# A hybrid attention block with fewer, wider transfers, eight places for the raw differential values, and broadcasts finished later

## The chip, the cores and the metric

The kernel runs on one core of a Trainium2 chip. TensorE (PE) multiplies; VectorE (DVE), ScalarE (ACT) and GpSimd (POOL) do the element-wise work; SyncE (SP) only issues DMAs, and ACT issues some too. Each engine works through its own list of instructions in order and waits on semaphores. The metric is the device time of one execution in microseconds (us), the median of three runs. Times inside an execution are microseconds from the start of the profiled span.

## The reference

The block works on one sequence of 1024 rows and 1024 channels, all float32. One input norm and one wide projection feed two attention branches, which gates merge:

```python
h = rms_norm(x, norm_in); proj = h @ w_in
(dq, dk, dv, dgate, cq, ckv, kr, mgate, g_diff, g_mla) = jnp.split(proj, split_idx, axis=-1)
# differential branch: 4 heads, two maps of 64 each, values 128 wide
dq, dk = apply_rope(dq), apply_rope(dk)
o_diff = causal_multimap_attention(dq, dk, dv, [1, -lam], 64 ** -0.5)
o_diff = rms_norm(o_diff, diff_subln) * (1 - lambda_init) * silu(dgate)
# latent branch: 4 heads, 128 + 64 rope; cq is 384 wide, ckv 256
q = rms_norm(cq, mla_q_norm) @ w_uq;  kv = rms_norm(ckv, mla_kv_norm) @ w_ukv
o_mla = causal_multimap_attention(concat(q_nope, rope(q_rope)), concat(k_nope, rope(kr)), mv) * silu(mgate)
merged = sigmoid(g_diff) * (o_diff @ w_proj_diff) + sigmoid(g_mla) * (o_mla @ w_proj_mla)
return rms_norm(x + merged @ w_out, norm_final)
```

## The kernel before, in words

Every product of two float32 matrices is made of three matmuls (`mm3`, L158 to L161): each operand is split into a rounded high part and the remainder as a low part (`split`, L150: ACT casts, then DVE or POOL subtracts), and high×high, high×low and low×high are summed in PSUM.

**Start, 0 to 67 us.** The raw differential values are made first: eight steps over blocks of 128 channels (order `KORD`), each with 24 matmuls into eight PSUM banks (`psd`, L216). After the last step each bank is copied by ACT into a tile of the tag `t`, which has four places (L391, L392), and stored by a DMA that ACT issues too (`d_dr`, L393). The rows of x are loaded meanwhile (`load_row`, L302) and squared on ACT for the input norm.

**Units, 67 to 486 us.** The rest of the wide projection is 19 units (`unit`, L470), each of which makes two column blocks of 128 for all 1024 rows by Strassen's seven products of 12 matmuls. `weights` (L342) builds the seven combinations of a unit's weights from four raw tiles (`wr`, loaded at L339; six places). The results go through sinks: rotation and split and store (`sink_rope`), gates (`sink_gate`, `sink_silu`), raw latent columns (`sink_c`). `store_split` (L562) writes the high part into a tile `uh` and the low part into `ul`, with two places each, and stores each by a DMA of its own. Between the products *chores* are called from a list: rope tables of one half (`rope_half`, L678), blocks of the differential values (`dv_block`, L724), and the latent norm's scaling (`latent_norm`, L632). A row of scale factors is broadcast over the partitions by `spread` (L613): POOL writes a diagonal into a `uh`, `ul` pair, and 9000 ns of the program's own count later (`defer`, L630) PE multiplies it by ones into the bank `tp`. That happens for the input norm's two halves (`rbc`) and for four latent jobs.

**Heads, 486 us to the end.** `load_stacks` (L879) loads a differential head's queries and keys as six tiles of 128 partitions, by twelve DMAs of 64 partitions each; `load_dv` (L891) loads its values and gate. Then come scores, softmax and the product with the values; the latent branch's tiles (`ch`, `cl`, `cosm`, `sinm`, `krh`, `krl`, L1001 on) are loaded after the first head's. The merge, the output projection and the last norm end the kernel.

A scheduler lays out the instructions of each engine from this program before it runs; the order in a queue is therefore not the order of the lines. The DMAs of SP and ACT share eight completion semaphores (`DMAHW0` to `DMAHW7`) in turn. A DMA whose semaphore still belongs to an earlier DMA is issued only after that one has landed, and the issuing engine's later instructions stand behind it.

## Time and profile before

| | us |
|---|---|
| median of 3 runs (955.65 to 956.18) | 955.98 |
| the profiled execution | 959.97 |
| its span | 958.2 |
| PE busy in it | 870.7 |
| DVE busy | 658.1 |
| POOL busy | 431.3 |
| ACT busy | 391.6 |

The profiled execution is 1.77 us longer than its span. PE is busy in 91% of the span, at a mean granted clock of 0.954 of full speed; a busy PE is not always a PE at full clock, so a stretch is read by its busy time and its granted clock together. In a row of waits, "A <- B" reads: A stood idle until B was done. In the timeline an idle time ahead of an instruction and what ended it stand in brackets.

### The profile page before, as it was taken

Reading aid. Unit: us, or ns where it says so; the run is one execution under the profiler, and the core shown is the slowest. Engines: PE = TensorE matmul, PEld = TensorE weight load, DVE = VectorE, ACT = ScalarE, POOL = GpSimd, SP = SyncE. Lnnn points to the kernel's source line nnn. Section 1 sums busy time; section 2 is a strip of 40 time slices with the busy share of each in tenths; the row PEclk is TensorE's granted clock in tenths of the full one; section 3 lists DMA queues with packets and bytes.
Section 4 is the critical chain, followed back from the end, with each engine's and each line's share of the span. In section 5 each row is a group of like instructions: output and inputs, shape, how many; then the busy total and the mean of one; then the engine's idle time right before and its main releaser. Section 6 shows DMA issues by size and latency. Waiting matters only on the chain.

```text
span 958.2 us, 12234 instructions
## 1 busy us (share of the span) xinstructions
PE 870.7 (91%) x4100; PEld 713.1 (74%) x4100; DVE 658.1 (69%) x1080; ACT 391.6 (41%) x768; POOL 431.3 (45%) x345
## 2 busy tenths in 40 slices
PE   8939899978798999999948899997999889999997
PEld 6727688756576878888835688886889658888886
DVE  7928666899989798866527568688587557554242
ACT  7563443233242333344315356565465443222211
POOL 6755345866756665545406533436243722220001
PEclk9969999979988999999978799999999999999999
DMA  7362332479583333332379621634131357444051
GB/s 275 115 242 77 110 113 96 133 230 283 200 270 136 108 134 119 123 111 99 95 205 383 151 72 63 148 104 123 49 122 55 109 175 232 134 132 165 19 182 64
DMA packets 71967, 137.92 MB, mean 144 GB/s; under 512 B 7904, under 2 KB 18912, under 8 KB 71904
## 3 DMA queue, kind: packets, MB, share of 16 engines
q1 hardware_dynamic: 64704, 124.16, 41.0%
q10 hardware_dynamic: 7200, 12.98, 3.7%
q8 instruction: 32, 0.52, 0.2%
q14 instruction: 31, 0.25, 0.1%
HBM read 91.76 MB, written 45.35 MB: 143 GB/s over the span
## 4 chain that ended last, share of the span: by engine, by line
PE 50%; DVE 5%; DMA 4%; ACT 3%; POOL 1%; issue 1%; SPq 0%; POOLq 0%; DVEq 0%; ACTq 0%
PE mm L159 9%; PE mm L161 9%; PE mm L160 9%; PE acc L161 3%; PE acc L159 3%; PE acc L160 3%; PE pv L160 2%; DVE sc L815 2%; PE mm L833 2%; PE sc L919 1%; PE pv L161 1%; PE pv L159 1%; PE sc L920 1%; DMA or<-d_od 1%; PE sc L1115 1%
## 5 line engine op out<-in xcount | busy, mean ns | idle before, releaser
L152 POOL TENSOR_TENSOR wl<-ws,wh 128x512 fp32r<-128x512 f32 x57 | 83.6, 1476 | 80.3 <-ACT wh L151 50.0
L815 DVE CUSTOM_DVE_ANT_0 sc<-sc,mask 128x128 f32<-128x128 f32 (+7 forms) x96 | 72.7, 763 | 30.6 <-PE sc L920 16.8
L152 POOL TENSOR_TENSOR wl<-wr,wh 128x512 fp32r<-128x512 f32 x45 | 64.0, 1421 | 36.9 <-ACT wh L151 32.0
L352 POOL TENSOR_TENSOR ws<-wr,wr 128x512 f32<-128x512 f32 x38 | 56.8, 1495 | 43.4 <-issue 22.2
L151 ACT CAST wh<-ws 128x512 fp32r<-128x512 f32 x76 | 46.8, 618 | 66.8 <-PE mm L160 61.6
L817 ACT ACTIVATE e<-sc,mn 128x128 f32<-128x128 f32 (+3 forms) x64 | 47.6, 745 | 34.2 <-DVE mn L815 22.5
L151 ACT CAST uh<-c 128x512 fp32r<-128x512 f32 x35 | 21.6, 619 | 88.0 <-DVE c L559 44.6
L159 PE MATMUL acc<-woh,mh 128*128 128x512 f32 (+1 forms) x136 | 51.3, 377 | 0.0
L161 PE MATMUL acc<-woh,ml 128*128 128x512 f32 (+1 forms) x136 | 51.3, 377 | 0.0
L160 PE MATMUL acc<-wol,mh 128*128 128x512 f32 (+1 forms) x136 | 51.3, 377 | 0.0
L152 POOL TENSOR_TENSOR wpl<-wpr,wph 128x512 fp32r<-128x512 f32 x16 | 21.8, 1365 | 62.2 <-ACT wph L151 62.2
L151 ACT CAST wh<-wr 128x512 fp32r<-128x512 f32 x64 | 39.5, 617 | 23.8 <-PE mm L160 11.5
L919 PE MATMUL sc<-kh,qs 128*128 128x512 f32 (+2 forms) x96 | 39.0, 410 | 11.1 <-DMA kh<-d_qk 8.2
L931 POOL TENSOR_SCALAR eb<-eb,rs 128x128 f32<-128x128 f32 (+5 forms) x24 | 17.1, 711 | 67.7 <-DVE rs L927 53.7
L159 PE MATMUL mm<-b11h,wh 128*128 128x512 f32 x76 | 33.1, 436 | 14.8 <-ACT t L392 14.8
L1129 POOL TENSOR_SCALAR e<-e,rs 128x128 f32<-128x128 f32 (+5 forms) x24 | 16.6, 696 | 56.4 <-DVE rs L1125 52.8
L1319 POOL TENSOR_TENSOR r<-s,nhalf 128x1 f32<-128x1 f32 x7 | 3.8, 544 | 83.9 <-DVE s L1317 81.7
L833 PE MATMUL mm<-ident,e 128*128 128x128 f32 x200 | 37.0, 281 | 2.7 <-DVE part L1210 1.2
L152 DVE TENSOR_TENSOR ul<-c,uh 128x512 fp32r<-128x512 f32 x35 | 36.5, 1045 | 3.7 <-DMA d_qk<-ul 1.8
L352 DVE TENSOR_TENSOR ws<-wr,ws 128x512 f32<-128x512 f32 x19 | 25.6, 1346 | 18.5 <-POOL wl L152 18.5
L920 PE MATMUL sc<-kl,qs 128*128 128x512 f32 (+2 forms) x96 | 34.3, 364 | 4.3 <-DMA kl<-d_qk 4.3
L152 DVE TENSOR_TENSOR pl<-mm,ph 128x512 fp32r<-128x512 f32 (+2 forms) x56 | 34.0, 610 | 5.7 <-ACT ph L151 5.3
(337 smaller groups left out, 2937.6 us busy)
## 6 DMA issues: line engine op xcount, KB each, us to landing
wr<-in_w_t SPq DMA_DIRECT2D x76, 256.0 KB, 3.0
d_t<-c ACTq DMA_DIRECT2D x32, 256.0 KB, 2.1
tg<-d_t SPq DMA_DIRECT2D x32, 256.0 KB, 3.0
big<-in_x SPq DMA_DIRECT2D x8, 512.0 KB, 5.6
d_qk<-uh SPq DMA_DIRECT2D x16, 256.0 KB, 2.3
d_qk<-ul SPq DMA_DIRECT2D x16, 256.0 KB, 2.6
qs<-d_qk SPq DMA_DIRECT2D x16, 256.0 KB, 6.1
kh<-d_qk SPq DMA_DIRECT2D x16, 256.0 KB, 6.9
```

Of the source, the lines that this page charges most:

```text
L151: A.copy(hi, src)
L152: (eng or V).tensor_tensor(lo, src, f32(hi), op=ALU.subtract)
L159: T.matmul(ps, lhsT=lh, rhs=rh, start=first, stop=False, skip_group_check=skip)
L160: T.matmul(ps, lhsT=lh, rhs=rl, start=False, stop=False, skip_group_check=skip)
L161: T.matmul(ps, lhsT=ll, rhs=rh, start=False, stop=last, skip_group_check=skip)
L352: eng.tensor_tensor(t, p_, q, op=op)
L815: V.tensor_tensor_reduce(sc[:, 0:W], sc[:, 0:W], mask[:, S - W:S], scale=-scale, scalar=BIG, op0=ALU.add, op1=ALU.min, accum_out=mn)
L817: A.activation(dst, sc[:, 0:W], AF.Exp, scale=-1.0, bias=mn, accum_out=sm)
L833: T.transpose(tp[:, blk(j)], pr[j][:, blk(kb)], ident)
L919: T.matmul(sc[:, c0:c0 + n], lhsT=q, rhs=kh[m][:, c0:c0 + n], start=True, stop=False)
L920: T.matmul(sc[:, c0:c0 + n], lhsT=q, rhs=kl[m][:, c0:c0 + n], start=False, stop=True)
L931: G.tensor_scalar(eb[:, 0:W], eb[:, 0:W], r, 0.0, op0=ALU.mult, op1=ALU.add)
```

## The change

Transfers are merged. Two blocks of `w_dv` and both halves of a `w_t` weight come by one DMA each into `wr` tiles of twice the width, three places in the place of six. The high and the low part of a result lie side by side in one tile `uhl` (two places), and one DMA stores both, in DRAM layouts that keep them together (`d_c`, `d_q`, `d_k`, `d_dv`, `d_rope`). A head's queries and keys come by six DMAs of 512 KB, its values by one, its gate by one; the latent tiles by one each for high and low. SP's list goes from 430 to 318 rows.

The list of PSUM banks of the first stage is reversed. Copies 4 to 7 of the raw values go into tiles of the tag `c` (six places), so that the eight copies have eight places. The subtraction for `s4` stands two steps earlier in `weights`. The second half of a broadcast is deferred by 13000 in the place of 9000. The count of instructions on PE, DVE, ACT's arithmetic and POOL stays the same but for the order.

```diff
-    d_dv = [one(dram, [4, P, NB - 1, P], F32, f"d_dv{i}") for i in range(2)]
-    d_df = one(dram, [4, P, 2, P], F32, "d_df")
+    d_dv = one(dram, [4, P, 16, P], F32, "d_dv")
     d_dr = one(dram, [NB, P, 512], F32, "d_dr")
-    d_c = [one(dram, [6, P, S], F32, f"d_c{i}") for i in range(2)]
+    d_c = [one(dram, [P, 2, S], F32, f"d_c{i}") for i in range(6)]
     d_cr = one(dram, [5, P, S], F32, "d_cr")
-    d_qk = [one(dram, [4, P, S], F32, f"d_qk{h}") for h in range(4)]
+    d_qk = [[one(dram, [P, 2, S], F32, f"d_{x}{h}") for x in "qk"] for h in range(4)]
     d_dg = one(dram, [4, P, S], F32, "d_dg")
-    d_rope = one(dram, [2, P, S], F32, "d_rope")
+    d_rope = one(dram, [P, 2, S], F32, "d_rope")
     d_od = one(dram, [4, P, S], F32, "d_od")
...
-    psd = [mk(ps0, [P, 512], F32, "bank", 8) for _ in range(NB)]
+    psd = [mk(ps0, [P, 512], F32, "bank", 8) for _ in range(NB)][::-1]
...
-    def load_x(k):
-        wr = mk(pw, [P, 512], F32, "wr", 6)
+    wrs = {}
+
+    def load_wd(i):
+        wrs[i] = mk(pw, [P, 2, 512], F32, "wr", 3)
+        return wrs[i]
+
+    def load_x(s):
+        k = KORD[s]
         xt = mk(p0, [P, S], F32, "big", 6)
...
+            if s % 2 == 0:
+                nc.sync.dma_start(load_wd(s // 2), a["w_dv"][s // 2::4].rearrange("k p c -> p k c"))
...
+        return wrs[s // 2][:, s % 2], xt
+
+    loaded = [load_x(s) for s in range(5)]
     V.memset(ones, 1.0)
...
-    def load_w_raw(u, which):
+    def load_w_raw(u, i):
         if u < len(plan):
-            for i, hf in which:
-                t = mk(pw, [P, 512], F32, "wr", 6)
-                nc.sync.dma_start(t.rearrange("p (k c) -> p k c", k=4), a["w_t"][plan[u][i]][:, 4 * hf:4 * hf + 4])
-                raw_w[u, i, hf] = t
+            t = raw_w[u, i] = mk(pw, [P, 2, 512], F32, "wr", 3)
+            nc.sync.dma_start(t.rearrange("p h (k c) -> p (h k) c", k=4), a["w_t"][plan[u][i]])
...
         for u in range(len(plan)):
-            a11, a21, a22, a12 = (raw_w.pop((u, *x)) for x in ((0, 0), (1, 0), (1, 1), (0, 1)))
-            load_w_raw(u + 1, ((0, 0), (1, 0)))
+            w1, w2 = (raw_w.pop((u, i)) for i in range(2))
+            a11, a12, a21, a22 = w1[:, 0], w1[:, 1], w2[:, 0], w2[:, 1]
+            load_w_raw(u + 1, 0)
             yield out("b11", a11, V)
...
             yield out("t2", s2, G)
+            s4 = new(a12, s2, ALU.subtract, V)
             yield out("b21", a12, G)
             s3 = new(a11, a21, ALU.subtract, G)
-            load_w_raw(u + 1, ((1, 1), (0, 1)))
+            load_w_raw(u + 1, 1)
             yield out("t3", s3, G)
...
             yield out("t4", a22, G)
-            s4 = new(a12, s2, ALU.subtract, V)
             yield out("b22", s4, V)
...
             if s == KD - 1:
-                raw = tmp()
+                raw = tmp() if b < 4 else mk(pst, [P, 512], F32, "c", CB)
                 last_copy[0] = A.copy(raw, psd[b]).ins
...
             all_chores()
-            load_w_raw(0, ((0, 0), (1, 0), (1, 1), (0, 1)))
+            load_w_raw(0, 0)
             for b in range(2):
...
             all_chores()
+            load_w_raw(0, 1)
             chores.extend([lambda b=b: square_row(b) for b in range(2)])
...
-    def store_split(src, hi_d, lo_d):
-        hi = mk(pst2, [P, 512], F32R, "uh", 2)
-        lo = mk(pst2, [P, 512], F32R, "ul", 2)
-        split(hi, lo, src)
-        nc.sync.dma_start(hi_d, f32(hi))
-        nc.sync.dma_start(lo_d, f32(lo))
-
-    def sink_rope(hi_d, lo_d):
+    def pair_tile():
+        return mk(pst2, [P, 2, 512], F32R, "uhl", 2)
+
+    def store_split(src, dst, eng=None):
+        hl = pair_tile()
+        split(hl[:, 0], hl[:, 1], src, eng)
+        nc.sync.dma_start(dst, f32(hl))
+
+    def sink_rope(dst):
         def sink(n, src, owned):
...
             def last():
-                store_split(box["g"], hi_d[:, half(n)], lo_d[:, half(n)])
+                store_split(box["g"], dst[:, :, half(n)])
                 drop()
...
         fl = mk(pst2, [P, 4], F32R, "fl", 2)
-        dg = [mk(pst2, [P, 512], F32R, x, 2) for x in ("uh", "ul")]
+        hl = pair_tile()
+        dg = [hl[:, i] for i in range(2)]
         fn = f[:, 4 * n:4 * n + 4]
...
             use(b)
-        defer(9000, finish)
+        defer(13000, finish)
...
             V.tensor_scalar(r, r, rstd[:, b:b + 1], None, op0=ALU.mult)
+            rv = r.rearrange("p (h c) -> p h c", h=4)
             if b % 4 == 3:
-                nc.sync.dma_start(d_df[:, :, b // 4, :].rearrange("h p c -> p h c"), r.rearrange("p (h c) -> p h c", h=4))
+                nc.sync.dma_start(d_dv[:, :, 14 + b // 4, :].rearrange("h p c -> p h c"), rv)
             if b < NB - 1:
-                hi = mk(pst2, [P, 512], F32R, "uh", 2)
-                lo = mk(pst2, [P, 512], F32R, "ul", 2)
-                split(hi, lo, r)
-                for i, v in enumerate((hi, lo)):
-                    nc.sync.dma_start(d_dv[i][:, :, b, :].rearrange("h p c -> p h c"),
-                                      f32(v).rearrange("p (h c) -> p h c", h=4))
+                hl = pair_tile()
+                split(hl[:, 0], hl[:, 1], r)
+                for i in range(2):
+                    nc.sync.dma_start(d_dv[:, :, 7 * i + b, :].rearrange("h p c -> p h c"),
+                                      f32(hl[:, i]).rearrange("p (h c) -> p h c", h=4))
             drop()
...
     def load_stacks(h):
-        st, kh, kl = stacks[h] = [[mk(pD, [P, S], F32R, f"{x}{m}", 1) for m in range(2)] for x in ("qs", "kh", "kl")]
-        src = d_qk[h]
-        for m in range(2):
-            own, other = slice(64 * m, 64 * m + 64), slice(64 - 64 * m, 128 - 64 * m)
-            nc.sync.dma_start(f32(st[m][own]), src[0][own])
-            nc.sync.dma_start(f32(st[m][other]), src[1][own])
-            for t, s_ in ((kh, src[2]), (kl, src[3])):
-                nc.sync.dma_start(f32(t[m][own]), s_[own])
-                nc.sync.dma_start(f32(t[m][other]), s_[own])
+
+        q = mk(pD, [P, 2, S], F32R, "qs", 1)
+        k = mk(pD, [P, 2, 2, S], F32R, "ks", 1)
+        for x in range(2):
+            r = slice(64 * x, 64 * x + 64)
+            nc.sync.dma_start(f32(q[r]), d_qk[h][0].rearrange("(m r) i s -> i r m s", m=2)[x])
+            for i in range(2):
+                nc.sync.dma_start(f32(k[r, i]), d_qk[h][1].rearrange("(m r) i s -> i r m s", m=2)[i])
+        stacks[h] = [[t[:, m] for m in range(2)] for t in (q, k[:, 0], k[:, 1])]
 
     def load_dv(h):
-        vh = mk(pD, [P, NB - 1, P], F32R, "dvh", 1)
-        vl = mk(pD, [P, NB - 1, P], F32R, "dvl", 1)
-        vf = mk(pD, [P, 2, P], F32, "dvf", 1)
-        nc.sync.dma_start(f32(vh), d_dv[0][h])
-        nc.sync.dma_start(f32(vl), d_dv[1][h])
-        nc.sync.dma_start(vf, d_df[h])
-        dvs[h] = vh, vl, vf
+        v = mk(pD, [P, 16, P], F32R, "dv", 1)
+        nc.sync.dma_start(f32(v), d_dv[h])
+        dvs[h] = v[:, 0:7], v[:, 7:14], f32(v[:, 14:16])
+        u = mk(pD, [P, S], F32, "du", 1)
+        nc.sync.dma_start(u, d_dg[h])
         for g in range(2):
-            dgate[h, g] = mk(pD, [P, 512], F32, "du", 2)
-            nc.sync.dma_start(dgate[h, g], d_dg[h][:, half(g)])
+            dgate[h, g] = u[:, half(g)]
...
     pL = pool("pL", "left")
-    cos = one(pL, [P, S], F32, "cosm")
-    sin = one(pL, [P, S], F32, "sinm")
-    ch = [one(pL, [P, S], F32R, f"ch{c}") for c in range(5)]
-    cl = [one(pL, [P, S], F32R, f"cl{c}") for c in range(5)]
-    krh = one(pM, [P, S], F32R, "krh")
-    krl = one(pM, [P, S], F32R, "krl")
+    rope = one(pL, [P, 2, S], F32, "rope")
+    cos, sin = rope[:, 0], rope[:, 1]
+    chl = [one(pL, [P, 2, S], F32R, f"chl{c}") for c in range(5)]
+    ch, cl = ([t[:, i] for t in chl] for i in range(2))
+    krhl = one(pM, [P, 2, S], F32R, "krhl")
+    krh, krl = krhl[:, 0], krhl[:, 1]
...
-    def load_c(c):
-        for t, d in ((ch, d_c[0]), (cl, d_c[1])):
-            nc.sync.dma_start(f32(t[c]), d[c])
-
-    load_c(3)
-    load_c(4)
+    for c in (3, 4):
+        nc.sync.dma_start(f32(chl[c]), d_c[c])
     load_latent_w(0)
-    nc.sync.dma_start(f32(krh), d_c[0][5])
-    nc.sync.dma_start(f32(krl), d_c[1][5])
     for c in range(3):
-        load_c(c)
-    nc.sync.dma_start(cos, d_rope[0])
-    nc.sync.dma_start(sin, d_rope[1])
+        nc.sync.dma_start(f32(chl[c]), d_c[c])
+    nc.sync.dma_start(f32(krhl), d_c[5])
+    nc.sync.dma_start(rope, d_rope)
```

ACT's list at the end of the first stage, before, with what each instruction waits for (`bank` are the PSUM banks, `t` the four places, `big` the rows of x):

```order
62 L392 COPY t_573<-bank_170 128x512 [waits PE_49]
63 L392 COPY t_583<-bank_171 128x512 [waits PE_49]
64 L392 COPY t_589<-bank_172 128x512 [waits DMAHW3_49,PE_49]
65 L393 DMA d_dr<-t_573 128x512 [waits DMAHW6_49,Activation_49]
66 L393 DMA d_dr<-t_583 128x512 [waits DMAHW7_49,Activation_49]
67 L393 DMA d_dr<-t_589 128x512 [waits DMAHW0_49,Activation_49]
68 L151 CAST wh_648<-ws_642 128x512 [waits PE_49,Pool_49]
69 L392 COPY t_595<-bank_173 128x512 [waits DMAHW5_49]
70 L393 DMA d_dr<-t_595 128x512 [waits DMAHW1_49,Activation_49]
71 L392 COPY t_601<-bank_174 128x512 [waits DMAHW6_49]
72 L392 COPY t_607<-bank_175 128x512 [waits DMAHW7_49]
```

The copies in rows 64, 69, 71 and 72 wait for a DMA semaphore, that of the store that empties their place. After, where `bank_181` to `bank_174` are the same eight results in the same order, ACT's list reads:

```order
62 L403 COPY t_566<-bank_179 128x512 [waits PE_49]
63 L403 COPY t_576<-bank_178 128x512 [waits PE_49]
64 L404 DMA d_dr<-t_566 128x512 [waits DMAHW6_49,Activation_49]
65 L404 DMA d_dr<-t_576 128x512 [waits DMAHW7_49,Activation_49]
66 L403 COPY c_582<-bank_177 128x512 [waits PE_49]
67 L403 COPY c_588<-bank_176 128x512 [waits PE_49]
68 L403 COPY c_594<-bank_175 128x512 [waits PE_49]
69 L404 DMA d_dr<-c_582 128x512 [waits DMAHW1_49,Activation_49]
70 L404 DMA d_dr<-c_588 128x512 [waits DMAHW2_49,Activation_49]
71 L404 DMA d_dr<-c_594 128x512 [waits DMAHW3_49,Activation_49]
72 L403 COPY c_600<-bank_174 128x512 [waits PE_49]
```

The copies of the fifth to eighth bank no longer wait for a DMA semaphore; the stores of the third and the fourth stand ahead of them and wait for `DMAHW6` and `DMAHW7`.

DVE's list in the second unit, before (`r` are tiles of the rope table's second half, L484 and L488 two sums of the unit):

```order
83 L684 CAST r_250_1063<-r_252_1065 128x512
84 L152 TENSOR_TENSOR wl_932<-ws_929,wh_931 128x512
85 L685 TENSOR_SCALAR r_249_1062<-r_250_1063,ropec 128x512
86 L687 TENSOR_SCALAR r_251_1064<-r_249_1062 128x512
87 L688 TENSOR_SCALAR r_251_1064<-r_251_1064 128x512
88 L484 TENSOR_TENSOR u_945<-mm_900,u_882 128x512
89 L690 SCALAR_TENSOR_TENSOR r_249_1062<-r_251_1064,r_249_1062 128x512
90 L152 TENSOR_TENSOR wl_965<-wr_746,wh_964 128x512
91 L692 SCALAR_TENSOR_TENSOR r_250_1063<-r_251_1064,r_249_1062 128x512
92 L488 TENSOR_TENSOR c_977<-mm_947,u_945 128x512
```

The CAST stands nine rows ahead of the sum of L488. DVE's list there after (L495, L499 and L504 are L484, L488 and L493 of before):

```order
82 L495 TENSOR_TENSOR u_910<-mm_888,u_870 128x512
83 L362 TENSOR_TENSOR ws_991<-wr_737,ws_966 128x512
84 L152 TENSOR_TENSOR wl_926<-wr_737,wh_925 128x512
85 L499 TENSOR_TENSOR c_951<-mm_912,u_910 128x512
86 L725 TENSOR_TENSOR crs<-r_213_948,rbc 128x512
87 L727 TENSOR_TENSOR srs<-r_214_949,rbc 128x512
88 L504 TENSOR_TENSOR c_980<-mm_953,u_910 128x512
89 L697 CAST r_246_1093<-r_248_1095 128x512
90 L698 TENSOR_SCALAR r_245_1092<-r_246_1093,ropec 128x512
91 L700 TENSOR_SCALAR r_247_1094<-r_245_1092 128x512
```

The conversion of the positions (CAST) and what follows it stood ahead of the unit's sums and now stands behind them.

SP's list at the first head, before:

```order
226 L884 DMA qs_988_4165<-d_qk_82 64x1024 [waits DMAHW1_49]
227 L885 DMA qs_988_4165<-d_qk_82 64x1024 [waits DMAHW2_49]
228 L887 DMA kh_990_4167<-d_qk_82 64x1024 [waits DMAHW3_49,PE_49]
229 L888 DMA kh_990_4167<-d_qk_82 64x1024 [waits DMAHW4_49]
230 L887 DMA kl_992_4169<-d_qk_82 64x1024 [waits DMAHW6_49]
231 L888 DMA kl_992_4169<-d_qk_82 64x1024 [waits DMAHW7_49]
232 L884 DMA qs_989_4166<-d_qk_82 64x1024 [waits DMAHW0_49]
233 L885 DMA qs_989_4166<-d_qk_82 64x1024 [waits DMAHW1_49]
234 L887 DMA kh_991_4168<-d_qk_82 64x1024 [waits DMAHW2_49]
235 L888 DMA kh_991_4168<-d_qk_82 64x1024 [waits DMAHW3_49]
236 L887 DMA kl_993_4170<-d_qk_82 64x1024 [waits DMAHW4_49]
237 L888 DMA kl_993_4170<-d_qk_82 64x1024 [waits DMAHW5_49]
```

Every one of the twelve waits for the landing of the DMA that last had its semaphore. SP's list there after (`ks` holds what `kh` and `kl` held):

```order
157 L898 DMA qs_4019<-d_q_84 64x2x1024 [waits DMAHW4_49,PE_49]
158 L900 DMA ks_4020<-d_k_85 64x2x1024 [waits DMAHW5_49]
159 L900 DMA ks_4020<-d_k_85 64x2x1024 [waits DMAHW6_49]
160 L898 DMA qs_4019<-d_q_84 64x2x1024 [waits DMAHW7_49]
161 L900 DMA ks_4020<-d_k_85 64x2x1024 [waits DMAHW1_49]
162 L900 DMA ks_4020<-d_k_85 64x2x1024 [waits DMAHW2_49]
163 L905 DMA dv_4027<-d_dv 128x2048 [waits DMAHW3_49,PE_49]
```

Twelve loads have become six of twice the size, each with a wait for one semaphore of the eight.

## Rows read from the trace of the kernel before

**Rows 1.** The page, part 1: busy us, share of the span, instructions
```profile
PE 870.7 (91%) x4100; PEld 713.1 (74%) x4100; DVE 658.1 (69%) x1080; ACT 391.6 (41%) x768; POOL 431.3 (45%) x345
```

**Rows 2.** Waits of PE over the whole span: us in total, times, longest us
```profile
PE mm L159 <- ACT t L392: 14.8, 1, 14.8
PE sc L919 <- DMA kh<-d_qk: 8.2, 1, 8.2
PE tp L627 <- POOL uh L622: 7.4, 3, 2.9
PE mm L159 <- DVE c L488: 6.0, 2, 4.4
```

**Rows 3.** Timeline of ACT, 49 to 72 us: start, us, what, idle before
```profile
56.21 1.06 ACT L392 COPY t<-bank 128x512 f32<-128x512 f32 x2
...
57.67 1.07 ACT L392 COPY t<-bank 128x512 f32<-128x512 f32 x2 [0.40 <-ACT t L392]
63.07 0.59 ACT L392 COPY t<-bank 128x512 f32<-128x512 f32 x1 [4.33 <-DMA d_dr<-t]
...
66.29 1.07 ACT L392 COPY t<-bank 128x512 f32<-128x512 f32 x2 [0.40 <-ACT t L392]
```

**Rows 4.** Waits of SP's DMA queue, 45 to 60 us
```profile
SPq L339 <- DVE wl L152: 10.5, 1, 10.5
```

**Rows 5.** DMA issues, 48 to 66 us: KB each, median us to landing
```profile
big<-in_x SPq DMA_DIRECT2D x6, 512.0 KB, 5.9
```

**Rows 6.** Timeline of DVE, 104 to 118 us
```profile
109.78 0.43 DVE L684 CAST r<-r 128x512 f32<-128x512 int32 x1 [3.44 <-DMA r<-in_positions]
...
116.37 0.68 DVE L488 TENSOR_TENSOR c<-mm,u 128x512 f32<-128x512 f32 x1
```

**Rows 7.** Stretches: length; busy us (count) of five engines; PEclk, DMA share, GB/s
```profile
67.00:71.00 4.00, 4.00 (x10) 3.13 (x11) 0.48 (x1) 4.00 (x8) 1.28 (x1) 0.50 0.74 238
117.10:122.40 5.30, 5.30 (x13) 4.16 (x14) 5.13 (x8) 2.23 (x4) 1.41 (x1) 0.50 0.25 94
171.10:300.80 129.70, 111.66 (x437) 86.68 (x436) 119.74 (x165) 43.12 (x76) 88.03 (x58) 0.90 0.66 212
300.80:319.60 18.80, 18.80 (x79) 15.45 (x78) 13.95 (x17) 7.81 (x13) 9.82 (x7) 0.93 0.35 123
501.00:526.50 25.50, 22.23 (x81) 15.14 (x81) 17.83 (x53) 15.10 (x37) 15.24 (x16) 0.79 1.04 389
```

**Rows 8.** Waits of all engines, 171 to 301 us
```profile
ACT uh L151 <- DMA d_qk<-uh: 6.3, 3, 3.8
ACT uh L151 <- DMA d_dv<-uh: 6.0, 4, 3.2
```

**Rows 9.** DVE by line, 171.1 to 300.8 us: busy us, mean ns, idle before
```profile
L152 DVE TENSOR_TENSOR ul<-c,uh 128x512 fp32r<-128x512 f32 x28 | 28.4, 1017 | 3.3 <-DMA d_qk<-ul 1.8 <-ACT uh L151 0.9 <-DMA d_dv<-ul 0.3
...
L488 DVE TENSOR_TENSOR c<-mm,u 128x512 f32<-128x512 f32 x5 | 3.4, 680 | 0.0
```

**Rows 10.** Chain that ended last, 484 to 528 us: start, us, what
```profile
485.82 3.42 DMA d_t<-c
...
492.31 7.91 DMA kl<-d_qk
500.35 0.56 PE sc L920
```

**Rows 11.** DMA issues, 474 to 487.5 us
```profile
d_t<-c ACTq DMA_DIRECT2D x3, 256.0 KB, 2.7
kl<-d_qk SPq DMA_DIRECT2D x2, 256.0 KB, 3.5
```

**Rows 12.** Timeline of ACT, 474 to 487 us
```profile
483.10 0.33 ACTq L525 DMA_DIRECT2D d_t<-c  x1
```

**Rows 13.** Timeline of SP's DMA queue, 484.5 to 530 us
```profile
510.90 0.42 SPq L1029 DMA_DIRECT2D cl<-d_c  x1
```

**Rows 14.** Line 1029 (the latent loads), its last row
```profile
DMA to landing us min/median/max: 6.9/7.9/10.2
```

38 lines of the change are left out of this document (20 added, 18 removed).

## The prediction

> **What bounds the kernel now.** I read the page's busy times first: PE works in 870.7 of 958.2 us [rows 1], so 87.5 us of the span are PE's idle time, and no other engine comes near it. The list of PE's waits comes next: it says which waits a change can take away. Four rows hold most of what this change touches: one wait of 14.8 us for a copy of a PSUM bank by ACT (L392), one of 8.2 for a head's keys, 7.4 in three waits for the diagonals of a broadcast, and 6.0 in two for a sum by DVE (L488) [rows 2]. Beside the idle time PE loses time at half clock: after a long wait the granted clock reads 0.50 (1.2 GHz) for some microseconds, as at 67 to 71 and at 117.1 to 122.4 [rows 7]. So I go place by place, each with the timeline of the engine that PE waits for.
>
> **The change part by part.** All sums go against the profiled execution's own 959.97 us.
>
> *A, the drain of the first stage.* PE stops at 52.1 and starts at 66.9; the seventh of the eight copies releases it. The timeline of ACT shows why that is late: four copies run in pairs at 56.21 and 57.67, then the fifth stands 4.33 us until a store has landed and freed a place, and the last pair follows only at 66.29, with stores issued in between [rows 3]. With eight places no copy waits for a place. I lay out the new sequence: a start at 56.21, since the casts ahead of it keep their order; seven copies at 1.06/2 = 0.53 make 3.7; two pauses of 0.40 for the issue of stores, as the one in the rows, make 0.8; the release costs some 0.1. PE starts at 60.8, that is 6.1 earlier; I count 6. What can spoil it stands in ACT's new list: the stores of banks 3 and 4 are issued ahead of copy 5, and they wait for two semaphores of row loads. Such a load took 5.9 us to land here [rows 5]. In the kernel before, the row loads stood on SP behind a weight load that waited 10.5 us for DVE [rows 4]; in SP's new list six of them stand ahead of that weight load. If they go as late as before all the same, the two stores wait until about 59 to 60, and copies 5 to 7 bring PE back at 62 to 64: the gain is then 3 to 5. If ACT gets to the copies 2 us sooner, it is 8. The reversed list of banks I cost at nothing: in both orders the first product takes the bank that is copied seventh, so the bank that PE waits for is the same.
>
> *B, the second unit.* PE waits for L488, which stood in DVE's list nine rows behind the conversion of the positions; that conversion stood 3.44 us for its DMA, and the sum came only at 116.37 [rows 6]. The broadcast's later finish puts the conversion behind the unit's first two sums. The two waits for L488 are 6.0 [rows 2]. The half-clock stretch behind the longer is 5.3 us [rows 7], and at full clock would take half, so 2.6 more can go: 8.6 at the most. The table's arithmetic does not go away; it lands on the next sums, while DVE is not full there. I take 6.0; bounds 2 (the short wait stays and the moved conversion holds one later sum for as long as its 3.44) and 8.6.
>
> *C, the units from 171 to 301 us.* Here the broadcasts of the latent norm make PE wait 7.4 us for POOL's diagonals [rows 2], and the deferral of 13000 gives POOL 4 us more; the longest of those waits is 2.9, so they should go. But DVE is busy 119.7 of the 129.7 us of this stretch [rows 7], and none of its work is dropped. PE's waits that go here come back as waits for DVE, except where work moves to the stretch behind, in which DVE has 13.95 of 18.8 us [rows 7]. Counting DVE's instructions from the opening sum of the fifth unit to that of the tenth, some ten move out; at 119.74/165 = 0.73 us that is 7 us, of which 5 fit into the free 4.85 behind and the rest is late there. I count 2. Downwards: the high and low tiles had two places each, and ACT already stood 6.3 and 6.0 us for them [rows 8]. A pair is now free only when both halves have landed, and a broadcast holds one of two pairs through its whole deferral. A doubling of those 12.3 us, nearly all passed on to PE, is −10. Upwards +8, all of the 7.4 and a little clock.
>
> The mean of a subtraction with both inputs in SBUF is 1017 ns here, that of the sum whose first input is in PSUM 680 ns [rows 9]; so about a third of the former is a delay by something else, and POOL is busy 88 of the 129.7 us [rows 7]. The Trainium skill (SBUF — State Buffer, the section on the shared GpSimd and Vector port) says that a DVE operation with two SBUF inputs and a GpSimd operation take turns on one port pair, each holding it for its whole instruction. The trace agrees with it as far as these two means go. By that rule POOL's work, of which none is removed, goes on stretching DVE's, and C is 0 instead of 2: the sum is then 2 less.
>
> *D, the first head.* The chain of waits shows it whole: a store of ACT issued at 485.82 lands 3.42 us later, only then can SP issue the second map's loads, and the last key load, issued at 492.31, lands 7.91 us later; the scores go on at 500.35 [rows 10]. The new list has six loads, the last on the semaphore of the store that ACT issued at 483.10 [rows 12]; at the 2.7 us of such a store [rows 11] it is issued near 485.8, some 6.5 sooner than the last of the twelve. Its duration has no row: a 64-partition load of 256 KB took 3.5 in a quiet stretch [rows 11]; twice the bytes take between 3.5 and 7.0; I take 5, nearer the lower end, since a 128-partition load of 512 KB took 5.9 in a full one [rows 5]. So the keys are there at 490.8, some 9.5 us earlier. After it the stretch belongs to the DMAs: from 501 to 526.5 they run at a share of 1.04 and 389 GB/s [rows 7]. What must arrive before the last query product is the head's values and gate, the kr tile, two gate halves, five latent tiles and four weights, 8.6 MiB or 9.06 MB: 23.3 us at 389 GB/s, from 490 to 513. In the kernel before, the last latent tile was issued at 510.90 [rows 13] and landed up to 10.2 later [rows 14], at 521. So this limit is 8 us earlier and the softmax chain 9.5; the smaller counts, 8. Bounds: 4 (loads that share the DMAs take 7 us or more, and the chain is held at the values) and 12.
>
> *The rest at nothing.* The wider weight loads keep the same bytes; PE's waits for weights in the units are small beside the ones named, and the raw tiles come a whole unit ahead. If that cover goes, it is about the 5.9 us of one late 512 KB load [rows 5]. From the second head on, the lists of all engines are nearly the same.
>
> Sum: 6 + 6 + 2 + 8 = 22, so 959.97 − 22 = 938.0 for a profiled execution. The runs' median lies 3.99 below it: 934.0.
>
> **The rivals.**
> 1. *More comes back in the units.* The waits for diagonals go and DVE's work moves into slack, A and D reach their upper ends: 8 + 7 + 6 + 11 = 32, or 924. For it: 87.5 us of idle PE and half-clock stretches that go with the waits. Against it: DVE at 92% of that stretch.
> 2. *Fewer transfers, but the same bytes.* A stays at 3 since ACT stands at the stores, B at 3, C at 0, D at 4 since six large loads share the DMAs that twelve small ones shared: 10, or 946. For it: the DMA share of 1.04. Against it: the second map's loads were issued late for a store [rows 10], not for full DMAs.
> 3. *Slower: two pairs are too few.* A latent broadcast holds one pair for 13 us of the program's count. ACT, in order, then stands at the next cast of a result with the casts of weights behind it; PE has two products in hand, 24 matmuls at 5.30/13/2 = 0.20 us (the row at half clock [rows 7], halved), 4.9 us, and then waits 8.1 us for each of four broadcasts, 32 us; with A, B and D kept at 20 the time is 956 + 12 = 968. It decides once a hold costs PE over 5 us. For it: the waits for `uh` that were there already [rows 8]. Against it: each of those was under 3.8, and two pairs pass eight results in a unit of 19 us with ease while no broadcast is open.
> 4. *It does not do what it says.* The reversal moves no bank, and later broadcasts change no order where PE waits: only D and half of A, 11, or 945; counted with rival 2.
>
> **How the numbers follow.** The forecast has 0.52 (928 to 941 by itself), rival 1 0.17, rivals 2 and 4 together 0.23, rival 3 0.08. The range leaves out the outer part of rival 1 and most of rival 3: 920 to 950. What a measurement of this kernel can tell from no change is about 0.2%, or 1.9 us. Faster takes the forecast, rival 1 and nearly all of rival 2, 0.91; same 0.02; slower 0.07, rival 3 but for a little.
>
> **What would show it.** A: the seventh copy ends near 61 and PE's wait at the first product is 8 to 9 us; no copy waits for a store. B: no wait for L499 (L488 before) over 2 us near 112. C: no wait for the diagonals in PE's list, DVE still above 90% of the stretch, and the wait of ACT for `uhl` not above some 20 us. D: the last key load lands near 490, PE's wait there is 4 us, and the last query product of the first head ends 8 us nearer to the units' end. Wrong it would be if ACT's waits for `uhl` pass on to PE, or if the stores in ACT's list hold the copies as long as the missing places did.

## The result, and the profile after

The changed kernel takes 945.7 us (943.31 to 947.78, 4 runs) against 956.08 for the kernel before in the same comparison: a ratio of 0.9879, 95% interval 0.9838 to 0.9919. It is faster by about 10 us; 22 were forecast. Its profiled execution took 945.21 us, with a span of 943.2. That is 14.8 us below the profile of before, more than the runs differ, because that profile was 4 us above its own median. A second profile of the kernel before (first experiment below) has a span of 952.4, and stretches are compared with that one here.

The page of the changed kernel, its busy times; the row answers to [rows 1]:

```profile
PE 869.8 (92%) x4100; PEld 711.7 (75%) x4100; DVE 645.7 (68%) x1080; ACT 391.3 (41%) x768; POOL 433.0 (46%) x345
```

PE does the same work, with 14 us less of idle time (73.4 against 87.5). PE's waits of the changed kernel (us in total, times, longest), against [rows 2]:

```profile
PE mm L161 <- DVE wl L152: 11.9, 6, 3.7
PE mm L159 <- ACT c L403: 8.4, 1, 8.4
...
PE sc L930 <- DMA ks<-d_k: 4.2, 1, 4.2
...
PE tp L640 <- POOL uhl L635: 2.9, 1, 2.9
...
PE cst L617 <- ACT t L612: 2.3, 2, 1.3
PE mm L159 <- ACT u L485: 2.3, 2, 1.8
...
PE mm L159 <- DVE c L499: 1.8, 2, 1.1
```

The wait at the drain is down from 14.8 to 8.4, the first wait for keys from 8.2 to 4.2 (and 4.3 more for their low parts, L920 of before, are gone), the waits for diagonals from 7.4 to 2.9. L499 is the old L488: 6.0 is down to 1.8. But a wait of 11.9 us for low parts of weights from DVE heads the list, and the rows for L612 and L485 are new.

To see where PE gains and loses, I cut each profile at five marks read from the timelines: the first product of the units on PE; DVE's opening sum of the fourth unit (L478, now L489); the first score on PE; the last query product of the first head; the end.

| us in the stretch | start and drain | units 1 to 3 | units 4 to 19 | first head | rest | span |
|---|---|---|---|---|---|---|
| before, first profile | 66.9 | 82.8 | 336.5 | 55.2 | 416.9 | 958.2 |
| before, second profile | 65.2 | 82.0 | 334.3 | 54.8 | 416.2 | 952.4 |
| changed | 58.2 | 83.3 | 335.7 | 47.2 | 418.8 | 943.2 |
| change against the second | −7.0 | +1.3 | +1.5 | −7.6 | +2.6 | −9.2 |

The marks tell that the change has two gains, at the drain and at the first head, and that all the rest lost some 5 us of them.

*The drain.* ACT's timeline of the changed kernel (start, us, what, idle before), against [rows 3]:

```profile
53.53 1.06 ACT L403 COPY t<-bank 128x512 f32<-128x512 f32 x2
...
55.07 1.07 ACT L403 COPY t<-bank 128x512 f32<-128x512 f32 x2 [0.48 <-ACT t L403]
...
56.58 1.07 ACT L403 COPY c<-bank 128x512 f32<-128x512 f32 x2 [0.44 <-ACT t L403]
...
57.54 0.60 ACT L403 COPY c<-bank 128x512 f32<-128x512 f32 x1
60.65 1.20 ACTq L404 DMA_DIRECT2D d_dr<-c  x2
61.90 0.59 ACT L403 COPY c<-bank 128x512 f32<-128x512 f32 x1 [3.75 <-issue]
```

Seven copies run from 53.53 to 58.14 with pauses of 0.4 to 0.5 where stores are issued. The stores of copies 3 and 4 did not hold copy 5. Those of copies 6 and 7, issued at 60.65, do hold the eighth until 61.90; PE doesn't wait for it. The copies began 2.7 us sooner than the 56.21 of before. Most of that is the start of this execution: PE stopped at 49.8 us here, at 52.1 in the first profile of before and at 50.4 in the second.

*The first head.* The chain of waits there (start, us, what), and of the last load of keys in the second profile of before, against [rows 10]:

```profile
474.12 2.60 DMA d_t<-c
476.74 5.09 DMA ks<-d_k
```

```profile
487.10 6.56 DMA kl<-d_qk
```

The last load of keys is issued at 476.74 when a store has landed, and takes 5.09 us, where 5 was estimated. It lands 4.6 us after the first score, in the second profile of before 12.2 us after it.

### The profile page after: what moved, and what is told of

It is laid out like the page before. It is cut to its first block, busy times and chain, and to the rows that moved or that the text cites. A ratio compares the mean times of both kernels' runs of the same rounds, so it can differ in the third digit from the quotient of the medians.

```text
span 943.2 us, 11993 instructions
## 1 busy us (share of the span) xinstructions
PE 869.8 (92%) x4100; PEld 711.7 (75%) x4100; DVE 645.7 (68%) x1080; ACT 391.3 (41%) x768; POOL 433.0 (46%) x345
## 4 chain that ended last, share of the span: by engine, by line
PE 50%; DVE 6%; DMA 3%; ACT 3%; POOL 1%; issue 1%; POOLq 0%; SPq 0%; DVEq 0%; ACTq 0%
PE mm L159 9%; PE mm L161 9%; PE mm L160 9%; PE acc L161 3%; PE acc L159 3%; PE acc L160 3%; DVE sc L828 2%; PE mm L846 2%; PE pv L160 2%; PE pv L159 1%; PE pv L161 1%; DMA omr<-d_om 1%; PE sc L929 1%; PE sc L930 1%; ACT eb L830 1%; PE sc L1119 1%
## 5 line engine op out<-in xcount | busy, mean ns | idle before, releaser
L151 ACT CAST uhl<-c 128x512 fp32r<-128x512 f32 x35 | 21.4, 619 | 80.3 <-DVE c L570 27.9
L362 DVE TENSOR_TENSOR ws<-ws,wr 128x512 f32<-128x512 f32 x19 | 26.2, 1377 | 35.0 <-POOL wl L152 30.0
L152 DVE TENSOR_TENSOR uhl<-c,uhl 128x512 fp32r<-128x512 f32 x35 | 34.6, 992 | 13.8 <-ACT uhl L151 13.5
L161 PE MATMUL mm<-b11h,wl 128*128 128x512 f32 x76 | 32.7, 431 | 11.9 <-DVE wl L152 11.9
L929 PE MATMUL sc<-ks,qs 128*128 128x512 f32 (+2 forms) x96 | 38.9, 408 | 4.9 <-ACT e L830 4.5
L159 PE MATMUL mm<-b11h,wh 128*128 128x512 f32 x76 | 32.7, 430 | 11.2 <-ACT c L403 8.4
L151 ACT CAST ph<-mm 128x512 fp32r<-128x512 f32 (+2 forms) x56 | 29.3, 524 | 22.7 <-PE mm L846 15.9
L535 ACT ACTIVATE c<-c 128x512 f32<-128x512 f32 x32 | 20.2, 632 | 44.1 <-DVE c L525 43.9
```

Source lines behind the costliest of these rows:

```text
L151: A.copy(hi, src)
L152: (eng or V).tensor_tensor(lo, src, f32(hi), op=ALU.subtract)
L159: T.matmul(ps, lhsT=lh, rhs=rh, start=first, stop=False, skip_group_check=skip)
L161: T.matmul(ps, lhsT=ll, rhs=rh, start=False, stop=last, skip_group_check=skip)
L362: eng.tensor_tensor(t, p_, q, op=op)
L535: A.activation(box["g"], box["g"], AF.Tanh, scale=0.5)
```

## The experiments

All were timed in three rounds beside the kernel before. The ratio is to that kernel, with its 95% interval.

| kernel | us | ratio | start and drain | units 1 to 3 | units 4 to 19 | first head | rest |
|---|---|---|---|---|---|---|---|
| before_again | 957.96 | 1.0005 (0.9982 to 1.0028) | 65.2 | 82.0 | 334.3 | 54.8 | 416.2 |
| unreversed | 941.98 | 0.9849 (0.9818 to 0.9879) | 59.5 | 84.3 | 334.5 | 47.4 | 418.5 |
| places4 | 946.85 | 0.9896 (0.9868 to 0.9924) | 62.8 | 82.5 | 336.1 | 44.4 | 418.5 |
| before_places8 | 955.46 | 0.9977 (0.9955 to 0.9998) | 59.7 | 77.0 | 337.5 | 55.4 | 423.4 |
| heads12 | 947.56 | 0.9875 (0.9859 to 0.9891) | 58.2 | 81.3 | 336.8 | 53.1 | 416.4 |
| defer9 | 942.5 | 0.9835 (0.9805 to 0.9866) | 58.1 | 83.7 | 333.5 | 46.5 | 417.4 |
| before_defer13 | 954.72 | 0.9952 (0.9936 to 0.9969) | 65.2 | 83.2 | 331.3 | 55.2 | 416.7 |
| own_diag | 942.42 | 0.9829 (0.9813 to 0.9846) | 58.2 | 80.8 | 333.9 | 47.1 | 419.0 |
| own_diag_defer9 | 942.12 | 0.9824 (0.9783 to 0.9865) | 58.3 | 83.0 | 333.8 | 45.6 | 419.2 |
| s4late | 949.39 | 0.991 (0.9885 to 0.9936) | 59.3 | 78.6 | 342.8 | 48.8 | 418.9 |
| wt4 | 954.55 | 0.9965 (0.9938 to 0.9992) | 59.5 | 87.3 | 333.7 | 48.2 | 423.1 |
| two_parts | 941.31 | 0.9829 (0.9788 to 0.987) | 59.9 | 76.9 | 335.9 | 44.4 | 418.8 |

**before_again.** No edit.

> The kernel before, once more, to see how much of a difference between two profiles is the execution's own. Theory: about 956 us in the runs, and its profile shows the same waits as the first profile within 0.3 us each (14.8 at the drain, 6.0 in two waits for the sum of L488, 8.2 for the keys); the 4 us by which the first profile was longer than the runs' median lie in waits for DVE in the units from 171 to 301 us. Rival: the waits move by a microsecond or more from one execution to the next, so that terms of 1 to 2 us cannot be told from one profile.

```profile
PE mm L159 <- ACT t L392: 14.8, 1, 14.8
...
PE mm L159 <- DVE c L488: 5.9, 2, 4.3
```

```profile
PE sc L919 <- DMA kh<-d_qk: 7.1, 1, 7.1
```

The first two of these waits of PE are the same as in [rows 2] within 0.1 us. The third, for the keys, was 8.2 there, and the waits for diagonals went from 7.4 to 6.1. So the theory holds for two of its three waits, and the rival for the other: waits for a DMA or for POOL moved by more than a microsecond. The spans differ by 5.8 us, 1.7 in the start, 0.9 and 2.2 in the units, 0.4 and 0.6 in the heads; a part of that is how long PE stays at half clock after a wait. So a term under 2 us can't be told from one profile. The runs of this kernel alone go from 954.02 to 960.98 us, which is wider than the 1.9 us that the prediction took as what can be told from no change.

**unreversed.** `psd = [mk(ps0, ...) for _ in range(NB)]` without `[::-1]`.

> The changed kernel with the list of PSUM banks not reversed. Theory: the reversal does nothing here, since the lists of all engines stay the same and the first product takes the bank that is copied seventh in both: 945.7 us within 2, PE idle 8.4 us at the drain. Rival: the bank that PE waits for is copied earlier or later; then the wait at the drain moves by 0.5 us for each copy (up to 3) and so does the time.

The wait at the drain is 7.4 against 8.4, and start and drain together take 1.3 more. The time is 3.7 below 945.7, outside the expected 2 us; since the lists are the same, that is how far two comparisons of one kernel lie apart (the two intervals overlap), and this kernel serves as the changed one's repeat. The reversal brings nothing that these runs can tell.

**places4.**

```diff
-                raw = tmp() if b < 4 else mk(pst, [P, 512], F32, "c", CB)
+                raw = tmp()
```

> The changed kernel with four places for the raw differential values in the place of eight. Theory (the places make the gain at the drain): copies 5 to 8 wait for stores again, PE's wait at the drain is 13 to 15 us against 8.4, and the time is 5 to 6 us longer, 951. Rival (the merged transfers make it, since the row loads go out earlier and the stores land sooner): the wait stays under 10 us and the time within 2 us of 945.7.

PE's wait of this kernel at the drain, and ACT's timeline there:

```profile
PE mm L159 <- ACT t L403: 12.9, 1, 12.9
```

```profile
56.95 0.58 ACT L403 COPY t<-bank 128x512 f32<-128x512 f32 x1 [0.81 <-DMA d_dr<-t]
60.56 0.58 ACT L403 COPY t<-bank 128x512 f32<-128x512 f32 x1 [3.03 <-DMA d_dr<-t]
```

Copies 5 and 6 wait for stores again, 0.81 and 3.03 us. The wait is 4.5 us longer than with eight places and 1.9 shorter than before: the places make 4.5 of the 6.4 us at the drain. The rest comes with the other edits; the fifth copy waits 0.81 us for its store and not the 4.33 of [rows 3], which fits the rows that are loaded sooner, but no run has these alone. The time is 946.85, the rival's, with an interval that overlaps the changed kernel's; in the profile the first head (44.4) gave back 2.8 of the 4.6 us lost up to the first product. The expected 951 was not reached.

**before_places8.** The kernel before with the changed kernel's line for eight places, `raw = tmp() if b < 4 else mk(pst, [P, 512], F32, "c", 6)`.

> The kernel before with eight places for the raw values as the only edit. Theory (places): PE's wait at the drain falls from 14.8 to 9 or 10 us, time 956 - 5 = 951. Rival (merged transfers): the stores of the third and fourth copy, which stand ahead of the fifth on ACT, wait for row loads that go out as late as before, the wait stays at 12 us or more and the time within 3 us of 956.

```profile
PE mm L159 <- ACT c L392: 9.4, 1, 9.4
```

The wait falls to 9.4 as the theory had it, and the first three units become 5 us shorter as well, with broadcasts still after 9000. Yet the time is 955.46: units 4 to 19 took 3.2 us more than in the second profile of before, and the rest of the kernel 7.2 more. The edit changed the lists of all engines to beyond 750 us. In the rest there are two waits of PE that the other kernels have not at this length (see wt4). The gain at the drain is real and does not reach the end by itself.

**heads12.**

```diff
-        for x in range(2):
-            r = slice(64 * x, 64 * x + 64)
-            nc.sync.dma_start(f32(q[r]), d_qk[h][0].rearrange("(m r) i s -> i r m s", m=2)[x])
+        for m in range(2):
+            own = slice(64 * m, 64 * m + 64)
+            for x in range(2):
+                r = slice(64 * x, 64 * x + 64)
+                nc.sync.dma_start(f32(q[r, m]), d_qk[h][0][own, x])
             for i in range(2):
-                nc.sync.dma_start(f32(k[r, i]), d_qk[h][1].rearrange("(m r) i s -> i r m s", m=2)[i])
+                for x in range(2):
+                    r = slice(64 * x, 64 * x + 64)
+                    nc.sync.dma_start(f32(k[r, i, m]), d_qk[h][1][own, i])
```

> The changed kernel with the six loads of a head's queries and keys cut into twelve of 256 KB again, from the new layouts. Theory (fewer DMAs wait for fewer landings): from the first score to the last query product of the first head it takes 54 to 55 us again, as in the kernel before (54.8), against 47.2 and 47.4 in the two profiles of the changed kernel; time 944 + 7 = 951. Rival (the DMAs were full anyway, and the gain came from the values, gate and latent tiles in one load each): 48 to 50 us, time within 2.5 of 944.

The chain of waits and PE's waits for keys of this kernel:

```profile
475.93 3.34 DMA d_t<-c
482.33 6.78 DMA ks<-d_k
```

```profile
PE sc L933 <- DMA ks<-d_k: 7.4, 1, 7.4
PE sc L934 <- DMA ks<-d_k: 3.8, 2, 2.4
```

The first score stands at 476.33 here, so the last key load goes out 6.0 us behind it (0.5 ahead of it in the changed kernel), and PE waits 11.2 us for keys instead of 4.2. The first head takes 53.1. The six loads make 5.9 of the 7.6 us; the other wide loads of that stretch are left with 1.7, which two profiles can't tell from 0. But the rest is 416.4 here, as in both profiles of before and in before_defer13 (416.2 to 416.9), and 417.4 to 419.2 in the kernels with six loads whose last heads are otherwise alike: some 2 us of the gain are given back later. That is not the order of the lists: from 536 us on, the four engines work through the same operations in the same order in both kernels. The rest of the changed kernel has 11.8 us at half clock, that of heads12 5.5; what brings that about stays open. In time it is 947.56, not the 951 expected.

**defer9 and before_defer13.** `defer(9000, finish)` in the changed kernel, and `defer(13000, finish)` in the kernel before.

> The changed kernel with the broadcasts finished after 9000 as before. Theory (the deferral only moves DVE's work, which is paid later): PE's waits for the diagonals come back, it is 5 to 10 us behind the changed kernel around 200 to 240 us, but the first score stands within 2.5 us of the changed kernel's 477.3 and 478.3, and the time within 3 us of 944. Rival (the deferral is worth what its waits cost): first score 5 us later or more, time 949 or more.

> The kernel before with the deferral of 13000 as the only edit. Theory (work moved, paid later): PE is 5 to 10 us ahead of the kernel before at some time between 195 and 240 us and gives it back by 370; first score within 2.5 us of 481.4 (of the second profile of before), time within 3 us of 957. In the second unit the wait of 4.3 us for the sum of L488 goes, and another wait with a half-clock stretch of 3 to 5 us comes in the first two units. Rival (the gain stays): first score at 475 or earlier, time 951 or less.

PE's waits of before_defer13 from the fourth unit to the first score, and those of the second profile of before in that stretch:

```profile
PE mm L161 <- DVE wl L152: 12.1, 6, 5.0
...
PE tp L627 <- POOL uh L622: 1.7, 1, 1.7
PE tp L628 <- POOL ul L622: 0.9, 1, 0.9
```

```profile
PE tp L627 <- POOL uh L622: 6.1, 3, 2.7
PE mm L159 <- ACT wh L151: 4.8, 3, 3.2
PE mm L161 <- DVE wl L152: 3.1, 3, 1.3
PE tp L628 <- POOL ul L622: 2.5, 1, 2.5
```

The later finish does what it is for: the waits for diagonals fall from 8.6 to 2.6 us. The wait for DVE's low parts of weights rises from 3.1 to 12.1 in the same stretch. In all, units 4 to 19 gain 3 us by it in the kernel before and lose 2.2 by it in the changed one (335.7 against 333.5 with 9000). The times say the same: before_defer13 is a little faster than before, defer9 is 942.5 against 941.98 and 945.7 of the changed lists. Counted by PE's matmuls, 84 to a unit, before_defer13 is 7.4 us ahead of the second profile of before at the start of the ninth unit, and 1.8 from the eleventh on. The theory holds: moved, not saved. A detail of it was wrong: in defer9 the diagonals' waits did not come back; others stood in their place, 6.1 us of them for a sum by DVE (L504).

before_defer13 is also the test of part B alone. The longer wait for L488, 4.3 us, is gone, but at the same place, 115 us, PE waits 2.3 us for low parts of weights, and the first three units take 83.2 us against 82.0. The later finish by itself brings nothing there.

**own_diag.**

```diff
-        hl = pair_tile()
-        dg = [hl[:, i] for i in range(2)]
+        if f is rstd:
+            hl = pair_tile()
+            dg = [hl[:, i] for i in range(2)]
+        else:
+            dg = [mk(pst2, [P, 512], F32R, x, 1) for x in ("r0", "r1")]
```

> The changed kernel with the diagonals of the four latent broadcasts in the tiles of the rope table (free by then) and not in a pair of the two for results. Theory (DVE's work is the limit between 190 and 340 us, not the places): the first score within 2 us of 477.3 and 478.3, time within 3 of 944. Rival (pairs held through the deferral make ACT and so PE wait): first score 4 us earlier or more, time 940 or less, and the waits for weights (wl by DVE, 11.9 us) fall by half.

```profile
PE mm L161 <- DVE wl L152: 10.2, 4, 3.2
```

The first score came at 472.9, 4.4 us earlier, which by itself would speak for the rival. But 2.5 of it was there before the first latent broadcast, where the lists are those of the changed kernel; units 4 to 19 took 333.9 against 335.7 and 334.5 of the two profiles with the changed lists. And the wait for low parts, which by the rival was to halve, is 10.2 against 11.9. So a pair held by a diagonal costs at most some 2 us, no more than two profiles differ by.

**own_diag_defer9.** Both edits.

> The changed kernel with both: the latent diagonals in tiles of their own, and the broadcasts finished after 9000. Theory (the held pairs cost some 4 us in the units, and the deferral is worth nothing): first score at 471 to 474 us, time 939 to 942. Rival (with a short hold the pairs are no limit, so the two edits take away the same wait): first score near the 475.3 of the kernel with the short deferral alone, time 942 to 943.

First score 475.1, time 942.12: the rival's case, nothing is added.

**s4late.**

```diff
-            s4 = new(a12, s2, ALU.subtract, V)
             yield out("b21", a12, G)
...
             yield out("t4", a22, G)
+            s4 = new(a12, s2, ALU.subtract, V)
```

> The changed kernel with the subtraction for s4 back in its late place. Theory (the same work of DVE in another order): the waits of PE for weights by DVE (11.9 us) change, the first score stays within 2.5 us of 477.3 and 478.3, time within 3 of 944. Rival (the early subtraction is what brings PE its weights in time): first score 480 or later, time 947 or more.

PE's waits of this kernel in units 4 to 19:

```profile
PE mm L161 <- DVE wl L152: 15.0, 5, 5.2
```

The theory falls, and the rival's numbers come. The late place is four steps of `weights` behind the early one (the text ahead of the prediction says two). It costs 7 us in units 4 to 19, with 15.0 us of waits for low parts, and gives 2 to 6 in units 1 to 3 (78.6 against 80.8 to 84.3 of the four kernels with the changed lists there). In time, 949.39, it is the slower place. The edit is one line, but the scheduler moved other instructions with it, on DVE up to 464 us, so the 7 us are those of the whole order.

**wt4.** Each `w_t` weight by two DMAs of 256 KB into the halves of its wide tile.

> The changed kernel with each weight of a unit loaded by two DMAs of 256 KB again, into the same wide tiles. Theory (PE hardly waits for these loads, so their number is worth nothing in the units): first score within 2.5 us of 477.3 and 478.3, time within 3 of 944. Rival (the wider loads are part of the gain, at the drain by the row loads that go out earlier): PE's wait at the drain 10 us or more against 8.4, time 947 or more.

```profile
PE mm L159 <- ACT c L404: 5.8, 1, 5.8
...
PE bank L161 <- DVE b21l L156: 2.2, 1, 2.2
```

Both were partly wrong. The wait at the drain is shorter (5.8), since the first stage itself ended later, after a wait of 2.2 us for DVE; together they took 59.5, as in the other kernels with eight places. Units 1 to 3 took 4 us longer, and the rest 4.3 longer. The kernel is at 954.55. The number of weight loads is thus not free, but what it changes is the order of all lists, down to 749 us. The rest loses as it does in before_places8: the longest two waits of PE there are 3.3 us for a rotated tile of DVE and 2.5 for a low part of the probabilities,

```profile
PE mm L159 <- DVE rt L1064: 3.3, 1, 3.3
PE mm L847 <- DVE pl L152: 2.7, 2, 2.5
```

in both kernels alike (L1059 and L833 there), and the rest has 16.8 us at half clock (17.2 there), against 11.8 in the changed kernel and 10.3 in the second profile of before.

**two_parts.** From the kernel before: the edit of before_places8, and `load_stacks` of the changed kernel with `d_qk` in its new layout, the sinks still storing high and low apart.

```diff
...
-        sinks[J_DQ + h] = sink_rope(d_qk[h][0], d_qk[h][1])
...
+        sinks[J_DQ + h] = sink_rope(d_qk[h][0][:, 0], d_qk[h][0][:, 1])
...
```

> The kernel before with two parts of the change alone: eight places for the raw values, and a head's queries and keys in six loads of 512 KB (with the layout in DRAM that they need); the weights, the pairs of high and low parts, the broadcasts, s4 and the latent loads stay as before. The lists of all engines up to the first head are those of the kernel before with eight places, which reached its first score at 474.2 us. Theory (these two parts hold what the whole change brings): first score at 474 to 476, 48 to 50 us from there to the last query product of the first head, time 939 to 946, not above the changed kernel. Rival (the merge of the other transfers is needed): first score 478 or later, or over 51 us to the last query product, and time 949 or more.

```profile
PE mm L159 <- ACT c L392: 9.0, 1, 9.0
PE tp L627 <- POOL uh L622: 7.7, 3, 3.3
```

Two parts of the change make 941.31 us, a ratio of 0.9829 (0.9788 to 0.987), against 0.9879 and 0.9849 for the two runs of the whole change's lists. It beats the kernel before clearly. That it beats the whole change is not shown: the intervals overlap. That the other parts are not needed is. Its first head takes even less, 44.4, and the waits for diagonals (7.7) are all still there.

## Why the prediction was right in direction and half wrong in size

The time lies in the range, and the sign was right. But the sum of 22 was twice what came, and 945.7 lies outside the 928 to 941 of the forecast itself: the range holds it by the part that was added for rival 2. By its own steps, against the second profile of before:

- **A, 6 counted: right.** The wait fell by 6.4, by the mechanism named; the stores ahead of copy 5 did not hold it. The reversal was rightly costed at nothing. The places alone give 4.5 to 5.4 of the 6.4 (places4, before_places8); the rest comes with the other edits, perhaps by the row loads that go out sooner, which I had only as a risk.
- **B, 6 counted: wrong, nothing came** (+1.3 by these two profiles; the four with the changed lists there lie at 80.8 to 84.3 against 82.0 and 82.8). The step that failed is that the two waits for L488 would go for good, since the table's arithmetic "lands on the next sums, while DVE is not full there". PE's waits of 5.9 us for L488 became 0.7, and 5.2 us of others stood up, most of them on ACT and a unit earlier. ACT's timeline in the changed kernel:

```profile
91.60 0.63 ACT L612 ACTIVATE t<-c 128x512 f32<-128x512 f32 x1 [5.82 <-DVE c L508]
...
92.77 1.28 ACT L721 ACT_TABLE_LOAD   x1
94.06 0.72 ACT L721 ACTIVATE r<-r,ropec 128x512 f32<-128x512 f32 x1
...
95.81 0.57 ACT L485 COPY u<-mm 128x512 f32<-128x512 f32 x1
```

ACT, in order, stood 5.82 us for a sum of DVE that had the table's arithmetic ahead of it, then did the sines with a table load of 1.28, and only then the copy (L485) that PE's next product needs. PE waited 1.8 for it after 2.3 for the squares of L612, and worked at half clock behind it:

```profile
96.40:101.70 5.30, 5.27 (x12) 4.13 (x13) 2.35 (x2) 0.62 (x2) 2.09 (x2) 0.50 0.41 142
141.50:477.30 335.80, 314.77 (x1345) 253.20 (x1344) 261.38 (x342) 118.85 (x203) 198.66 (x135) 0.97 0.48 158
477.30:524.40 47.10, 33.04 (x116) 23.55 (x115) 33.22 (x72) 22.55 (x52) 23.27 (x22) 0.75 1.02 322
```

The first of these stretches is 5.3 us at a granted clock of 0.50, as long as the one in [rows 7] at 117.1, which stood behind a wait of 4.4. The bounds of 2 to 8.6 left out that the waits could be handed on in full. before_places8 and two_parts got 5 us in this stretch without any deferral, so most of the 6 was there to be had, by another order; and before_defer13 shows that the later finish alone is not what brings it.
- **C, 2 counted: nothing came, and the reason held.** The prediction says that the waits which go come back as waits for DVE. In the second row of the stretches above, units 4 to 19, PE is busy for 314.77 us, against 315.73 in the second profile of before:

```profile
147.10:481.40 334.30, 315.73 (x1344) 255.18 (x1343) 275.24 (x342) 118.25 (x203) 198.61 (x134) 0.96 0.46 154
481.40:536.20 54.80, 34.64 (x116) 23.82 (x115) 31.06 (x72) 22.28 (x52) 22.50 (x22) 0.72 1.00 308
```

and PE's waits there in the changed kernel are

```profile
PE mm L161 <- DVE wl L152: 11.9, 6, 3.7
PE tp L640 <- POOL uhl L635: 2.9, 1, 2.9
...
PE mm L159 <- ACT wh L151: 1.2, 3, 0.6
...
PE tp L641 <- POOL uhl L635: 0.3, 1, 0.3
```

against 8.6 for diagonals and 3.1 for low parts before (shown with before_defer13; the 7.4 of the prediction leaves out the row for the low halves, L628). The 8.6 became 3.2, the 3.1 became 11.9. Counted by PE's matmuls, 84 to a unit, the changed kernel is 5.6 us ahead of the second profile of before at the start of the fourth unit, 17.2 at that of the eighth, and 4.2 from the fourteenth on: the gain was there and was given back. What failed is the 2 us for work moved into slack behind: nothing of it is left, −1.5 by these profiles, which two profiles can't tell from 0. From the fifth unit's opening sum to the tenth's, DVE has 151 instructions and works 85% of the time, where over 90% was the sign, against 166 and 92% in the second profile of before. DVE's busy time in units 4 to 19 fell by 14 us (275.24 to 261.38) with the same 342 instructions. Some 10 of them are one line, the subtraction for `s4` (busy us and mean ns stand behind its count; the second profile of before, then the changed kernel):

```profile
L352 DVE TENSOR_TENSOR ws<-wr,ws 128x512 f32<-128x512 f32 x15 | 20.7, 1379 | 1.2 <-POOL wl L152 1.2
```

```profile
L362 DVE TENSOR_TENSOR ws<-wr,ws 128x512 f32<-128x512 f32 x15 | 11.1, 742 | 0.3
```

In s4late it takes 1383 ns again, so its early place is what makes it short, and by s4late that place is worth 7 us here; the other edits took away as much. So DVE's total, from which I had argued by the 92%, does not say how long PE waits: the kernel before has the most of it and the least waits for low parts. What stands ahead in DVE's list does, as far as the timelines tell: before the longest of these waits, 3.7 us at 247.7, DVE had worked without a pause since 234. Rival 3, the pairs, did not come as a time: own_diag bounds the pairs that diagonals hold at 2 us. But its premise did: between those two opening sums ACT waited 33.6 us for stores out of pairs, where not above 20 was the sign and 12.3 stood before. What that costs PE no run takes apart.
- **D, 8 counted: right in size, 7.6, but not by the limit that set it.** The sixth load took 5.09 where 5 was estimated, the keys were there at 481.8, 4.6 us after the first score, where 4 was written, and six loads for twelve make 5.9 of it. I took 8 and not 9.5 because the loads behind the keys, at full DMAs, were to be the limit. The DMAs were full in both kernels, shares of 1.02 and 1.00 in the rows above. Yet the chain that ended last has no load behind the last key load in this stretch, in either; it goes by the scores and DVE's and ACT's softmax, and takes 42.6 us from the keys to the last query product, 42.5 in the second profile of before. So the whole gain is that the keys came 7.7 sooner after the first score. Against the first profile they came 9.4 sooner, as the 9.5 had it; that the sum's 8 is so near is in part luck.
- **The rest, 0 counted: wrong by 2.6.** heads12 has it back at 416.4, with the same lists of the engines from the first head's end on, and two_parts, whose other loads are narrow, has it at 418.8. So it goes with the six loads of queries and keys; how is open. And the weight loads were not free in the sense I gave them (wt4).

So rival 2's time (946) came by another way than its own: A and D in full, B, C and the rest at nothing or below.

## What to carry to other kernels

Where engines work in order and wait for each other, count a removed wait as a gain only when you can name what PE waits for next: at the drain and at the first head PE's next work was ready, and 14 us came; in the units another queue was as late, and a gain of 11 us halfway was given back by their end. An edit that reorders a scheduler's lists should be tried by parts: places and six loads alone made the whole gain, and places alone almost none. And take two profiles of the kernel before: a term of 2 us is not in one.

## What the hardware showed that I had not expected

The time that PE spends at half clock after a wait differs from one execution to the next with the same lists. After the drain, which took the same 14.8 us in both profiles of the kernel before, one was at 0.50 for 4.0 us and more [rows 7], the other in these stretches (length, busy us of the engines, granted clock, DMA share, GB/s):

```profile
65.20:68.20 3.00, 3.00 (x7) 2.42 (x8) 0.50 (x1) 3.00 (x6) 1.28 (x1) 0.50 0.91 311
68.20:71.00 2.80, 2.80 (x13) 2.26 (x13) 0.00 (x0) 2.80 (x7) 0.67 (x1) 0.99 0.05 19
```

It was back at full clock after some 3.0 us. Spans of the same kernel lay 5.8 us apart with its longest wait of PE equal to 0.1.

A DVE subtraction of one shape, with both inputs in SBUF, took 742 ns on average at one place in the list and 1379 or 1383 at another (the lines for `s4` above). What stretches it there no run takes apart.
